# One product per 128 tokens in a gated recurrence, and a reordered opening, in a two-block transformer kernel

## The chip, the cores and the metric

The kernel runs on one core of one Trainium2 chip. The metric is device microseconds of one execution: 2290.91, the median of three runs (2289.15 to 2291.92). The engines are TensorE (matrix products; PE in the rows, its weight loads PEld), VectorE (DVE), ScalarE (ACT), GpSimd (POOL) and SyncE (SP, which issues most loads). TensorE writes to PSUM, in banks of 128 x 512 fp32; ScalarE and VectorE read it from there.

## The reference

One sequence of 512 tokens, width 1024, passes through two blocks in fp32. The first block has a normalised input projection, a differential attention (4 heads of two 64-wide halves, rotary positions, block-causal mask) beside a banded attention (8 heads), a cross attention to 256 memory tokens and a gated feed-forward stage. The second has a top-k attention with a gating branch, a feed-forward stage with a short convolution, a gated linear recurrence (8 heads), and another such feed-forward stage. Two parts matter here:

```
q, k = rope(z[q cols]), rope(z[k cols])      # x1*cos - x2*sin, x2*cos + x1*sin
attn = softmax(q0 k0') - lam * softmax(q1 k1');  out = attn @ v

# recurrence, per chunk of 64 tokens, state S (128 x 128), b = cumsum(log g)
inter = (q * exp(b)) @ S
a[t,s] = sum_d q[t,d] * exp(b[t,d] - b[s,d]) * k[s,d]   for s <= t, else 0
out = a @ i + inter
S = exp(b_last) * S + (k * exp(b_last - b))' @ i
```

## The kernel before

Activations are kept transposed, features on the 128 partitions and the 512 tokens along the free dimension, in eight tiles. Each weight product is done in three passes of TensorE's rounded fp32 type (`mm3`, L131 to L133): activation and weight are split into a high and a low half, and high x high, high x low and low x high are summed in one PSUM bank. ScalarE makes the high half of a weight tile of 128 x 1024 (`whi`, L118), VectorE the low half (`wlo`, L119); two of each are kept, and three raw tiles (`wraw`), which SyncE loads 512 KB at a time. A step of a product generator (`fm`, features out, one bank for 24 products when its head is 1; `tm512`, tokens out) is three products. Weight products use four PSUM banks (`pg`).

A planner orders each engine's instructions when the kernel is built: by its own estimate of time it takes, of what is ready, what comes first in the program; work in a `high_priority` block comes ahead of other work, and `issue_after(ins)` keeps work behind an instruction on that instruction's engine. Attention and recurrence heads are written as generators whose stages are advanced one per round by `pipeline` (from L397 on); after each round `fill` issues some steps of the generators in `self.line`, so that weight products lie between the dependent stages.

The opening is `mix`. It splits x into halves (`xg`), sums the squares (`sumsq`, L235 for the sums, L229 for squares on GpSimd, L231 for squares on ScalarE), and starts the query products (four tiles, four banks at once). After 16 steps, column sums give the mean square (`pst`, L244), GpSimd its inverse root (`rs`, L260), and two products its broadcast (`psb`, L286). The evacuation of a query or key tile, `rope`, has four ScalarE copies of 32 partitions out of PSUM (L497), a product with cos (L498), a product with sin on GpSimd (L499), a sum (L500), then casts and differences into halves (`pack_q` L418 and L419, `pack_k` L429 and L430). Then come four key tiles, then the values (`tm512`), small constants and the bias of the second attention on GpSimd's DMA queue, and then 16 attention steps, each with scores, softmax, transposes and a product with the values. The filler of these is the second attention's values, its queries and keys, and the gate.

The recurrence is `recur`. For each head, six levels of masked scores are put together in a buffer `abuf` of two halves (one per head in turn): its lower and upper 64 partitions hold the two 64x64 diagonal blocks of each group of 128 tokens, all groups in 4 x 64 columns. The scores of the second chunk with the first (L1142) come from PSUM. ScalarE puts these and the upper diagonal blocks into a tile `B` (128 x 256, L1146 and L1147). The state is updated (`pu`, L1161), and the output product is one uninterrupted run of TensorE instructions per head (L1171, L1172, L1174): fp32 products, each of which the profile records as two. TensorE is given its operands by tile shape (rows x columns of its array), which the rows name as 64*64, 128*64 or 128*128.

Of the kernel before, what the change touches and what calls it, by code (L numbers as in the profile page):

```python
# [8 lines left out]
F32 = mybir.dt.float32  # L9
# [4 lines left out]
ALU = mybir.AluOpType  # L14
AX = mybir.AxisListType

P = 128
# [52 lines left out]
class Kern:  # L70
# [400 lines left out]
    def mix(self):  # L471
        nc, d = self.nc, self.d
        xs = [self.u(f"x{k}", "x") for k in range(KT)]
        w = d["w_in"]
# [10 lines left out]
        op = [self.split(xs[k], "xg", self.col("norm_mix_g", k)) for k in range(KT)]  # L485
        self.more_consts()
        cos, sin = self.u("cos", "c"), self.u("sin", "c")
        nc.sync.dma_start(cos, d["cos"])
        nc.sync.dma_start(sin, d["sin"])
        acc = self.sumsq(xs, sq_eng=nc.gpsimd)  # L490
        qa, ka = [], []

        def rope(dst, pack):
            def evac(n, ps):
                r, sw = self.u("rope", "y"), self.u("sw", "a")
                for b in range(0, P, 32):
                    nc.scalar.copy(sw[b:b + 32], ps[b ^ 32:(b ^ 32) + 32])  # L497
                nc.vector.tensor_tensor(r, ps, cos, op=ALU.mult)  # L498
                self.pmul = nc.gpsimd.tensor_tensor(sw, sw, sin, op=ALU.mult).ins  # L499
                nc.vector.tensor_tensor(r, r, sw, op=ALU.add)  # L500
                dst.extend(pack(r))
            return evac

        def tok(dst, nm):
            def evac(j, ps):
                t = self.u(nm, "g")
                nc.scalar.activation(t, ps, AF.Identity, scale=rst[:, j:j + 1])
                dst[j] = t
            return evac
# [7 lines left out]
            nc.gpsimd.tensor_tensor(t, t, rsb, op=ALU.mult)  # L517
        self.run(first)
        va = [None] * 4
        self.run(self.fm(w[4:8], op, rope(ka, lambda z: self.pack_k(z, "g"))))  # L520
        self.run(self.tm512(w[8:12], op, tok(va, "va")))

        lv = self.u("lv", "a")[:, :256]
        nc.sync.dma_start(lv, bass.AP(tensor=d["lam"].tensor, offset=d["lam"].offset, ap=[[0, P], [1, 256]]))
# [12 lines left out]
        nc.vector.tensor_scalar(g8, self.col("subln"), 1.0 - lam_init, None, op0=ALU.mult)  # L537

        e0, e1 = self.u("ext", "a")[:8, :384], self.u("ext", "a")[:8, :384]
        with self.tc.issue_after(self.pmul):  # L540
            nc.gpsimd.dma_start(e0[:, 383:384], d["rbr"][:, 0:1])
            nc.gpsimd.dma_start(e1, d["rbr"][:, 1:385])
        nc.vector.tensor_copy(e0[:, 0:383], e0[:, 383:384].to_broadcast([8, 383]))
# [8 lines left out]
        def step(h, i):  # L552
            W = P * (i + 1)
            if i == 0:
                st[h, "r0"] = self.small("r0", 4)
            r0 = st[h, "r0"]
            zs = [self.pad_q(qa[2 * h + c], 64 * c, i) for c in range(2)]
            yield
            es, sm = [], self.small("sm2", 2)
            mx = self.small("mx2", 2)  # L560
            for c in range(2):
                ps = self.ps.tile([P, T], F32, name="psa", tag="ps")
                self.score(ps, qa[2 * h + c], ka[2 * h + c], zs[c], i, W, False)
                nc.tensor.matmul(ps[:, W - CUT:W], self.identb, self.corner, start=False, stop=True)
                nc.vector.tensor_reduce(mx[:, c:c + 1], ps[:, :W], axis=AX.X, op=ALU.max)
                nc.vector.tensor_scalar(mx[:, c:c + 1], mx[:, c:c + 1], -0.125, None, op0=ALU.mult)
                e = self.u("ea", "a")
                nc.scalar.activation(e[:, :W], ps[:, :W], AF.Exp, bias=mx[:, c:c + 1], scale=0.125,
                                     accum_out=sm[:, c:c + 1])
                es.append(e)  # L570
            rc = self.small("rc2", 2)
            nc.vector.reciprocal(rc, sm)
            nc.vector.tensor_copy(r0[:, i:i + 1], rc[:, 0:1])

            cf = self.small("cf", 1)
            nc.vector.scalar_tensor_tensor(cf, rc[:, 1:2], nlam, sm[:, 0:1], op0=ALU.mult, op1=ALU.mult)
            at = es[0]
            nc.vector.scalar_tensor_tensor(at[:, :W], es[1][:, :W], cf, es[0][:, :W], op0=ALU.mult, op1=ALU.add)
            yield
            pt = self.pt.tile([P, T], F32, name="pta", tag="pt")  # L580
            for j in range(i + 1):
                nc.tensor.transpose(pt[:, j * P:j * P + P], at[:, j * P:j * P + P], self.ident)
            aT = self.u("aT", "a")
            nc.scalar.copy(aT[:, :W], pt[:, :W])
            yield
            if i == 0:
                st[h, "po"] = self.po.tile([P, T], F32, name="poa", tag="po")
            po = st[h, "po"]
            for j in range(i + 1):
                nc.tensor.matmul(po[:, i * P:i * P + P], aT[:, j * P:j * P + P], va[j][:, h * P:h * P + P],  # L590
                                 start=j == 0, stop=j == i)
            if i == 3:
                o = self.u("oa", "a")
                r3 = lambda a: a.rearrange("p (i e) -> p i e", i=4)
                nc.vector.tensor_tensor(r3(o), r3(po), r0[:, :, None].to_broadcast([P, 4, P]), op=ALU.mult)
                self.head_norm(o, 4)
                yield
                yield
                yah[h] = self.to_feature(o, "ya", g8)

        qb, kb, vb = [None] * 8, [None] * 8, [None] * 4
# [12 lines left out]
        def gate(which, tag):  # L614
            def evac(n, ps):
                z = self.u("zg", tag[n])
                nc.vector.tensor_tensor(z, ps, rsb, op=ALU.mult)
                nc.scalar.activation(z, z, AF.Tanh, scale=0.5)
                tg[which, n] = z
            return evac  # L620
# [11 lines left out]

        ybh = [None] * 4
        qk = self.fm(w[16:24], op, heads)
        self.line = [self.tm512(w[12:16], op, tok(vb, "vb")), qk, self.fm(w[24:32], op, gate("a", "g" * 8))]
        self.pipeline([step(h, i) for h in range(4) for i in range(4)], RATE["a"])
        self.finish(qk)
        self.line += [self.fm(d["w_up_a"], yah, merge("a")),
# [395 lines left out]
    def recur(self, xs):  # L1034
        nc, d = self.nc, self.d
        op = [self.split(xs[k], "hg", self.col("mix1", k)) for k in range(KT)]
        acc = self.sumsq(xs)
        w = d["c_in"]
# [23 lines left out]
        abuf = self.u("abuf", "c")  # L1062
        with self.tc.issue_after(self.rs):
            nc.gpsimd.memset(abuf, 0.0)

        it = {}
        on = [None] * 8
# [15 lines left out]
        def grow(ks, qs, dec, m):  # L1083

            v4 = lambda t: t.rearrange("p (n a m) -> p n a m", a=2, m=m)
            d2 = dec.rearrange("p (n a) -> p n a", a=2)
            w = [P, T // (2 * m), m]
            nc.vector.tensor_tensor(v4(ks)[:, :, 0], v4(ks)[:, :, 0], d2[:, :, 1:2].to_broadcast(w), op=ALU.mult)
            nc.vector.tensor_tensor(v4(qs)[:, :, 1], v4(qs)[:, :, 1], d2[:, :, 0:1].to_broadcast(w), op=ALU.mult)

        def head(h):
            hc = slice((h % 4) * P, (h % 4) * P + P)
            itok = [it[h // 4, j][:, hc] for j in range(4)]
# [6 lines left out]
            g = zf  # L1100
# [8 lines left out]
            dec, at, w = [g], 0, T  # L1109
# [8 lines left out]
            A = abuf[:, (h % 2) * 256:(h % 2) * 256 + 256]  # L1118
            for lv in range(7):
# [4 lines left out]
                n = 32 if lv else 64  # L1124
                ps = self.ps.tile([P, T], F32, name="pl", tag="ps")
                for c in range(8):
                    r, s = (c % 2) * 64, slice(c * 64, c * 64 + 64)
# [7 lines left out]
                else:  # L1135
                    r3 = lambda t: t.rearrange("p (j t) -> p j t", j=4)
# [3 lines left out]
            ps = self.ps.tile([P, T], F32, name="pl", tag="ps")  # L1140
            for j in range(4):
                nc.tensor.matmul(ps[:64, j * 64:j * 64 + 64], ks[:, j * P:j * P + 64], qs[:, j * P + 64:j * P + P],  # L1142
                                 start=True, stop=True)
            yield
            B = self.u("B", "a")[:, :256]
            nc.scalar.copy(B[:64], ps[:64, :256])  # L1146
            nc.scalar.copy(B[64:], A[64:])  # L1147
            grow(ks, qs, dec[6], 64)
            yield
            pt = self.pt.tile([P, T], F32, name="ptk", tag="pt")  # L1150
# [8 lines left out]
            for j in range(3):  # L1159
                s = slice(j * P, j * P + P)  # L1160
# [4 lines left out]
                                               op0=ALU.mult, op1=ALU.add)  # L1165
            yield
            po = self.po.tile([P, T], F32, name="poh", tag="po")
            lo, hi = slice(0, 64), slice(64, P)
            for j in range(4):
                s, t = slice(j * P, j * P + P), slice(j * 64, j * 64 + 64)  # L1170
                nc.tensor.matmul(po[lo, s], A[lo, t], itok[j][lo], start=True, stop=j == 0)  # L1171
                nc.tensor.matmul(po[hi, s], B[:, t], itok[j], start=True, stop=j == 0)  # L1172
                if j:
                    nc.tensor.matmul(po[:, s], qs[:, s], sl(j), start=False, stop=True)  # L1174
            o = self.u("ho", "y")
# [33 lines left out]
        def heads(h):  # L1209
            self.finish(ti[h // 4])  # L1210
            self.finish(fq[h])
            yield from head(h)
            out_head(h)
# [187 lines left out]
```

## Time and profile before

| what | value |
|---|---|
| median of three runs | 2290.91 us |
| profiled execution | 2289.7 us |
| its span, first to last instruction | 2287.9 us |
| VectorE busy | 1390.4 us, 61% |
| ScalarE busy | 912.3 us, 40% |
| GpSimd busy | 272.0 us, 12% |
| mean granted TensorE clock | 0.991 |

Busy time of TensorE is that of products in a pipeline whose ends are modelled: a product of 512 columns is shown with 0.39 us where the next one starts 0.23 later. So the cost of a product is read from the starts of two that follow each other. Idle times count only where the engine had nothing else to do, and "released by" names the instruction that came last.

### The profile page before, as it was taken

Reading aid. Unit: us, or ns where it says so; the run is one execution under the profiler, and the core shown is the slowest. Engines: PE = TensorE matmul, PEld = TensorE weight load, DVE = VectorE, ACT = ScalarE, POOL = GpSimd, SP = SyncE. Lnnn points to the kernel's source line nnn. Section 1 sums busy time; section 2 is a strip of 40 time slices with the busy share of each in tenths; the row PEclk is TensorE's granted clock in tenths of the full one; section 3 lists DMA queues with packets and bytes.
Section 4 is the critical chain, followed back from the end, with each engine's and each line's share of the span. In section 5 each row is a group of like instructions: output and inputs, shape, how many; then the busy total and the mean of one; then the engine's idle time right before and its main releaser. Section 6 shows DMA issues by size and latency. Waiting matters only on the chain.

```text
span 2287.9 us, 28921 instructions
## 1 busy us (share of the span) xinstructions
PE 2226.7 (97%) x11254; PEld 1808.5 (79%) x11254; DVE 1390.4 (61%) x2391; ACT 912.3 (40%) x1426; POOL 272.0 (12%) x360
## 2 busy tenths in 40 slices
PE   7899999999999999998999999999999999999997
PEld 6778777888888888777678888888877778888886
DVE  7576556766444333589876877633456646777534
ACT  5454443544323222462553544422322234444322
POOL 4212200000111100123230000000112210000001
PEclk9999999999999999999999999999999999999999
DMA  4423323522533333313213333333212123333333
GB/s 143 99 64 94 93 74 102 160 71 76 106 98 96 99 95 100 103 47 95 67 56 92 94 100 95 99 95 101 84 56 65 56 65 93 98 96 99 95 99 104
DMA packets 62536, 207.28 MB, mean 91 GB/s; under 512 B 8216, under 2 KB 12384, under 8 KB 62400
## 3 DMA queue, kind: packets, MB, share of 16 engines
q1 hardware_dynamic: 58368, 198.60, 28.7%
q0 software_dynamic: 2880, 5.79, 1.6%
q8 instruction: 88, 1.44, 0.3%
q10 hardware_dynamic: 1152, 1.05, 0.1%
q14 instruction: 48, 0.39, 0.1%
HBM read 201.74 MB, written 3.67 MB: 90 GB/s over the span
## 4 chain that ended last, share of the span: by engine, by line
PE 86%; DVE 9%; ACT 2%; issue 1%; POOL 1%; DMA 0%; SPq 0%; DVEq 0%; ACTq 0%; POOLq 0%
PE pg L131 26%; PE pg L132 25%; PE pg L133 25%; PE pl L1128 1%; DVE isc L925 1%; DVE wlo L119 1%; PE po L390 1%; DVE m L924 1%; PE ptr L378 1%; ACT whi L118 1%; DVE qhl L419 1%; DVE khh L429 1%; DVE isc L915 1%; PE poh L1172 1%; PE poh L1171 1%
## 5 line engine op out<-in xcount | busy, mean ns | idle before, releaser
L118 ACT CAST whi<-wraw 128x1024 fp32r<-128x1024 f32 (+1 forms) x368 | 386.0, 1049 | 737.6 <-PE pg L132 458.9
L119 DVE TENSOR_TENSOR wlo<-wraw,whi 128x1024 fp32r<-128x1024 f32 (+1 forms) x356 | 436.7, 1227 | 320.4 <-ACT whi L118 314.4
L131 PE MATMUL pg<-fg2h,whi 128*128 128x512 f32 x704 | 274.1, 389 | 0.0
L133 PE MATMUL pg<-fg2h,wlo 128*128 128x512 f32 x704 | 273.9, 389 | 0.0
L132 PE MATMUL pg<-fg2l,whi 128*128 128x512 f32 x704 | 273.9, 389 | 0.0
L131 PEld LDWEIGHTS pg<-fg2h,whi 128*128 128x128 f32 x704 | 132.2, 188 | 27.4
L133 PEld LDWEIGHTS pg<-fg2h,wlo 128*128 128x128 f32 x704 | 132.2, 188 | 27.4
L132 PEld LDWEIGHTS pg<-fg2l,whi 128*128 128x128 f32 x704 | 132.2, 188 | 27.4
L133 PE MATMUL pg<-m2h,wlo 128*128 128x512 f32 (+1 forms) x374 | 140.9, 377 | 0.6 <-DVE wlo L119 0.6
L131 PE MATMUL pg<-m2h,whi 128*128 128x512 f32 (+1 forms) x374 | 141.0, 377 | 0.0
L132 PE MATMUL pg<-m2l,whi 128*128 128x512 f32 (+1 forms) x374 | 140.8, 376 | 0.0
L131 PE MATMUL pg<-fgh,whi 128*128 128x512 f32 x352 | 137.3, 390 | 0.9 <-ACT whi L118 0.9
L133 PE MATMUL pg<-fgh,wlo 128*128 128x512 f32 x352 | 137.1, 389 | 0.0
L132 PE MATMUL pg<-fgl,whi 128*128 128x512 f32 x352 | 137.0, 389 | 0.0
L1021 DVE SCALAR_TENSOR_TENSOR yc<-zc,vecs,yc 128x511 f32<-128x511 f32 (+1 forms) x176 | 130.8, 747 | 2.7
L260 POOL TENSOR_TENSOR rs<-ms,mhalf 128x4 f32<-128x4 f32 (+1 forms) x11 | 12.0, 1090 | 943.4 <-DVE ms L247 585.1
L131 PE MATMUL pg<-xgh,whi 128*128 128x512 f32 x256 | 103.9, 406 | 7.1 <-ACT xgh L217 5.9
L1017 DVE TENSOR_TENSOR zc<-pg,rsb 128x512 f32<-128x512 f32 x88 | 60.5, 688 | 74.1 <-PE pg L133 74.1
L132 PE MATMUL pg<-xgl,whi 128*128 128x512 f32 x256 | 101.9, 398 | 0.5 <-DVE xgl L218 0.5
L133 PE MATMUL pg<-xgh,wlo 128*128 128x512 f32 x256 | 101.2, 395 | 0.0
L133 PEld LDWEIGHTS pg<-m2h,wlo 128*128 128x128 f32 x374 | 70.3, 188 | 13.6 <-DVE wlo L119 0.8
L131 PEld LDWEIGHTS pg<-m2h,whi 128*128 128x128 f32 x374 | 70.3, 188 | 13.0
(424 smaller groups left out, 4812.6 us busy)
## 6 DMA issues: line engine op xcount, KB each, us to landing
wraw<-in_ffn_up SPq DMA_DIRECT2D x88, 512.0 KB, 3.5
wraw<-in_ffn_down SPq DMA_DIRECT2D x48, 512.0 KB, 3.5
wraw<-in_w_gate_up SPq DMA_DIRECT2D x44, 512.0 KB, 3.5
wraw<-in_w_in SPq DMA_DIRECT2D x39, 512.0 KB, 3.6
wraw<-in_c_in SPq DMA_DIRECT2D x32, 512.0 KB, 3.5
wraw<-in_ab SPq DMA_DIRECT2D x29, 512.0 KB, 3.6
wraw<-in_w_down SPq DMA_DIRECT2D x22, 512.0 KB, 3.5
wraw<-in_w_ckv SPq DMA_DIRECT2D x16, 512.0 KB, 4.1
```

What stands on the lines that cost most here:

```text
L118: nc.scalar.copy(hi[:, p], raw[:, p])
L119: eng.tensor_tensor(lo[:, p], raw[:, p], hi[:, p], op=ALU.subtract)
L131: mm(out, w[0], x[0], start=start, stop=False)
L132: mm(out, w[0], x[1], start=False, stop=False)
L133: return mm(out, w[1], x[0], start=False, stop=stop).ins
L378: nc.tensor.transpose(pt[:, j * P:j * P + P], es[a][:, j * P:j * P + P], self.ident)
L390: nc.tensor.matmul(po[r, i * P:i * P + P], v[j][:, c0:c0 + 64], pts[a][:, j * P:j * P + P], start=j == 0, stop=j == i)
L419: self.nc.vector.tensor_tensor(t[b:b + 64], z[a:a + 64], t[a:a + 64], op=ALU.subtract)
L429: (self.nc.scalar.copy if a == b else self.nc.vector.tensor_copy)(t[b:b + 64], z[a:a + 64])
L915: nc.vector.scalar_tensor_tensor(a[:, :W], r[:, :W], s, a[:, :W], op0=ALU.mult, op1=ALU.add)
L1017: nc.vector.tensor_tensor(z, ps, rsb, op=ALU.mult)
L1021: nc.vector.scalar_tensor_tensor(y[:, sh:], z[:, :T - sh], self.col(f"cw{l}{j}", f), y[:, sh:], op0=ALU.mult, op1=ALU.add)
```

## The change

In the recurrence, a tile `AB` of 128 x 4 x 128 (two of them, for heads in turn, with one quadrant cleared once) replaces `B`. Three ScalarE copies put the two diagonal blocks and the block between them in place, and one 128x128 product per group replaces a 64x64 and a 128x64 one.

In the opening, the squares go from GpSimd to ScalarE. The evacuation of query and key tiles is put at high priority, and its product with sin goes from GpSimd to VectorE. The values are produced right behind the queries, then the first key tile; the other three key tiles become filler of the attention rounds. A head's first step makes sure that its key tile is issued. Two small loads on GpSimd's queue are tied to the inverse root in place of the rotary product.

```diff
-        acc = self.sumsq(xs, sq_eng=nc.gpsimd)
-        qa, ka = [], []
+        acc = self.sumsq(xs)
+        qa, ka = [None] * 8, [None] * 8
...
-                for b in range(0, P, 32):
-                    nc.scalar.copy(sw[b:b + 32], ps[b ^ 32:(b ^ 32) + 32])
-                nc.vector.tensor_tensor(r, ps, cos, op=ALU.mult)
-                self.pmul = nc.gpsimd.tensor_tensor(sw, sw, sin, op=ALU.mult).ins
-                nc.vector.tensor_tensor(r, r, sw, op=ALU.add)
-                dst.extend(pack(r))
+                with self.tc.high_priority():
+                    for b in range(0, P, 32):
+                        nc.scalar.copy(sw[b:b + 32], ps[b ^ 32:(b ^ 32) + 32])
+                    nc.vector.tensor_tensor(r, ps, cos, op=ALU.mult)
+                    nc.vector.tensor_tensor(sw, sw, sin, op=ALU.mult)
+                    nc.vector.tensor_tensor(r, r, sw, op=ALU.add)
+                    dst[2 * n:2 * n + 2] = pack(r)
...
-        self.run(self.fm(w[4:8], op, rope(ka, lambda z: self.pack_k(z, "g"))))
+        keys = [self.fm(w[4 + p:5 + p], op, rope(ka, lambda z: self.pack_k(z, "g")), p) for p in range(4)]
         self.run(self.tm512(w[8:12], op, tok(va, "va")))
+        self.run(keys[0])
...
-        with self.tc.issue_after(self.pmul):
+        with self.tc.issue_after(self.rs):
...
             if i == 0:
+                self.finish(keys[h])
...
-        self.line = [self.tm512(w[12:16], op, tok(vb, "vb")), qk, self.fm(w[24:32], op, gate("a", "g" * 8))]
+        self.line = keys[1:3] + [self.tm512(w[12:16], op, tok(vb, "vb")), keys[3], qk,
+                                 self.fm(w[24:32], op, gate("a", "g" * 8))]
...
+            ab = [self.cp.tile([P, 4, P], F32, name=f"ab{n}") for n in range(2)]
+            for t in ab:
+                nc.gpsimd.memset(t[64:, :, :64], 0.0)
...
-            B = self.u("B", "a")[:, :256]
-            nc.scalar.copy(B[:64], ps[:64, :256])
-            nc.scalar.copy(B[64:], A[64:])
+            AB = ab[h % 2]
+            r3 = lambda t: t.rearrange("p (j t) -> p j t", j=4)
+            nc.scalar.copy(AB[:64, :, 64:], r3(ps[:64, :256]))
+            nc.scalar.copy(AB[:64, :, :64], r3(A[:64]))
+            nc.scalar.copy(AB[64:, :, 64:], r3(A[64:]))
...
-                s, t = slice(j * P, j * P + P), slice(j * 64, j * 64 + 64)
-                nc.tensor.matmul(po[lo, s], A[lo, t], itok[j][lo], start=True, stop=j == 0)
-                nc.tensor.matmul(po[hi, s], B[:, t], itok[j], start=True, stop=j == 0)
+                s = slice(j * P, j * P + P)
+                nc.tensor.matmul(po[:, s], AB[:, j], itok[j], start=True, stop=j == 0)
```

## Rows read from the trace of the kernel before

**Rows 1.** The page, busy time by engine: us, share, instructions.
```profile
PE 2226.7 (97%) x11254; PEld 1808.5 (79%) x11254; DVE 1390.4 (61%) x2391; ACT 912.3 (40%) x1426; POOL 272.0 (12%) x360
```
**Rows 2.** Waits of TensorE, whole span: who for whom, us in total, times, longest.
```profile
PE pst L244 <- DVE sq L235: 3.9, 1, 3.9
PE pg L132 <- DVE wlo L119: 3.9, 3, 2.2
PE pg L131 <- DVE rope L498: 3.7, 2, 2.5
```
**Rows 3.** Stretches: length, busy us and count of PE, PEld, DVE, ACT, POOL; clock; DMA.
```profile
26.00:32.00 6.00, 6.00 (x20) 4.96 (x21) 3.17 (x15) 0.22 (x1) 1.01 (x1) 0.60 0.31 91
40.00:60.00 20.00, 20.00 (x88) 16.56 (x89) 15.75 (x21) 18.74 (x32) 9.08 (x12) 1.00 0.27 79
60.00:80.00 20.00, 13.88 (x48) 10.32 (x47) 18.64 (x32) 12.66 (x20) 6.30 (x6) 0.83 0.31 72
96.00:130.00 34.00, 32.87 (x177) 27.17 (x176) 18.37 (x56) 15.47 (x38) 5.91 (x14) 1.00 0.38 90
1632.00:1700.00 68.00, 67.10 (x575) 52.40 (x574) 43.62 (x91) 15.10 (x22) 14.88 (x26) 1.00 0.24 71
```
**Rows 4.** Timeline of TensorE, output products of the first and last head: start, us.
```profile
1675.17 0.39 PE L133 MATMUL pg<-whi,hgl 128*128 128x512 f32 x1
1675.49 0.43 PE L1171 MATMUL poh<-itok,abuf 64*64 64x128 f32 x2
...
1676.94 0.49 PE L1174 MATMUL poh<-S,qs 128*128 128x128 f32 x2
1677.36 0.43 PE L1171 MATMUL poh<-itok,abuf 64*64 64x128 f32 x2
...
1679.63 0.66 PE L1128 MATMUL pl<-qs,ks 128*64 128x32 f32 x16
...
1863.24 0.43 PE L1171 MATMUL poh<-itok,abuf 64*64 64x128 f32 x2
...
1867.21 0.48 PE L131 MATMUL pg<-yhh,whi 128*128 128x512 f32 x1
```
**Rows 5.** Timeline of TensorE, state update of the first head and what follows.
```profile
1670.52 0.83 PE L1161 MATMUL pu<-itok,kst 128*128 128x128 f32 x6
1671.28 0.66 PE L1128 MATMUL pl<-qs,ks 128*64 128x32 f32 x16
```
**Rows 6.** Instructions of tile B: durations in ns (least, median, most), starts, forms.
```profile
L1147 ACT COPY B<-abuf x8: 402/402/408, 1653.1 to 1853.5; 64x256 f32<-64x256 f32 x8
```
**Rows 7.** Timeline of TensorE in the opening, around the column sums and the queries' end.
```profile
20.83 0.39 PE L131 MATMUL pg<-xgh,whi 128*128 128x512 f32 x1
25.17 1.87 PE L244 MATMUL pst<-ones,sq 128*128 128x1 f32 x8 [3.95 <-DVE sq L235]
...
38.36 0.39 PE L133 MATMUL pg<-xgh,wlo 128*128 128x512 f32 x1
39.93 0.50 PE L131 MATMUL pg<-xgh,whi 128*128 128x512 f32 x1 [1.18 <-DVE rope L498]
```
**Rows 8.** Squares: on GpSimd (tile sq, opening), on ScalarE (by line, whole span).
```profile
L229 POOL TENSOR_TENSOR sq<-x x8: 1165/1494/1956, 5.1 to 21.5; 128x512 f32<-128x512 f32 x8
...
L231 ACT ACTIVATE sq<-x 128x512 f32<-128x512 f32 x48 | 28.7, 619 | 2.3 <-DVE sq L235 2.3
```
**Rows 9.** ScalarE by line, 36 to 60 us: busy us, mean ns, idle before.
```profile
L497 ACT COPY sw<-pg 32x512 f32<-32x512 f32 x24 | 13.9, 578 | 2.9 <-PE pg L133 2.5
L418 ACT CAST qhl<-rope 64x512 fp32r<-64x512 f32 x8 | 5.0, 619 | 0.9 <-DVE rope L500 0.7
L118 ACT CAST whi<-wraw 128x1024 fp32r<-128x1024 f32 x3 | 3.1, 1048 | 0.0
```
**Rows 10.** VectorE by line, 36 to 80 us.
```profile
L430 DVE TENSOR_TENSOR kl<-rope,khh 64x512 fp32r<-64x512 f32 x8 | 5.9, 733 | 0.2
L498 DVE TENSOR_TENSOR rope<-pg,cos 128x512 f32<-128x512 f32 x8 | 5.5, 689 | 3.9 <-ACT sw L497 3.7
```

More of the change, by code (lines that the diff above doesn't have):

```diff
@@ L1167, in head @@
             po = self.po.tile([P, T], F32, name="poh", tag="po")
-            lo, hi = slice(0, 64), slice(64, P)
             for j in range(4):
-                s, t = slice(j * P, j * P + P), slice(j * 64, j * 64 + 64)
-                nc.tensor.matmul(po[lo, s], A[lo, t], itok[j][lo], start=True, stop=j == 0)
-                nc.tensor.matmul(po[hi, s], B[:, t], itok[j], start=True, stop=j == 0)
+                s = slice(j * P, j * P + P)
+                nc.tensor.matmul(po[:, s], AB[:, j], itok[j], start=True, stop=j == 0)
                 if j:
```

## The prediction

> **What bounds the kernel now.** I read the busy times first: TensorE is busy for 97% of the span, no other engine for more than 61% [rows 1]. Next came the list of what TensorE waited for. Its rows for the opening are short ones: 3.9 us for the sum of squares, 3.9 us in three waits for the low halves of weights, 3.7 us in two waits for rotary products to let go of a PSUM bank [rows 2]. So time is to be had in two ways: fewer TensorE microseconds where it never waits, or those waits and the clock that falls after them. Then the stretches: in the recurrence (1632 to 1700 us) TensorE is busy 67.1 of 68 us at full clock, with VectorE at 43.6 and ScalarE at 15.1 [rows 3]. In the opening the granted clock is 0.60 in 26 to 32 us and 0.83 in 60 to 80 us, where it is 1.00 in the rest of what is shown: the lower of the two levels (1.2 GHz) for part of these stretches, each time behind a stretch in which TensorE stood still [rows 3, 7]. Last came the order of instructions on TensorE at the two places that the change edits [rows 4, 5, 7], and the durations of what moves [rows 6, 8 to 10].
>
> The sum is made against the profiled execution, 2289.7 us (span 2287.9 and 1.8 around it). It lies 1.2 below the median of the three runs, 2290.91; I put the difference on that median.
>
> **Recurrence: products.** Per head the output product is issued as one block. For each of four groups of 128 tokens it has a 64x64 product (L1171), a 128x64 product (L1172) and, in three groups, the 128x128 product with the state (L1174). Each is two records. The first head's block starts at 1675.49 and the next work starts at 1679.63: 4.14 us. The last head's goes from 1863.24 to 1867.21: 3.97 us [rows 4]. The six between show 4.14 or 4.15, so eight blocks are 7 x 4.14 + 3.97 = 32.95 us. In front of the block TensorE also loses a little: the full product at 1675.17 needs 0.23, the block comes 0.32 behind it, so 0.09 x 8 = 0.7. After the change a block has seven products, all 128x128 with 128 columns in fp32 (four of the score tile, three of the state). The nearest row is the state update of the same stage, three products of just that form: from 1670.52 to the start of the following work at 1671.28, 0.76 us, so 0.253 each with the change of shape at the end in it [rows 5]. Seven are 1.77, eight blocks 14.2. Gain: 32.95 + 0.7 - 14.2 = 19.5 us.
> Bounds: if every product were spaced like the state product that now stands before a smaller one, 0.42 (1676.94 to 1677.36) [rows 4], a block were 2.94 and the gain 9.4 (without the 0.7). If 0.16 of the 0.76 is the change of shape, a product is 0.20, a block 1.56 and the gain 21.2. I take 19.5, since rows 5 have the form itself.
> Is it on the path? TensorE has 0.9 us of idle in 68 there [rows 3], so what goes from it goes from the span. A round that had a block loses 2.4 us of cover for the other engines, but stays longer by 1.8 than the rounds without one, which have their cover now.
> The rows show the two half-width products of a group one behind the other (8 of them and 3 whole ones in 4.14). The Trainium skill, page "TensorEngine Tiling (Array Packing)", section "Tiling Modes", says that different tiles of the array can load weights and multiply in parallel; by that a 64x64 and a 128x64 product on different columns would share their time, and the sum would lose this whole term. The trace does not agree, with 4.14 for the block where seven whole products would be 1.77.
>
> **Recurrence: the rest.** Two ScalarE copies of 64x256 become three; the one from the score buffer takes 0.40 [rows 6], so 8 x 0.40 = 3.2 us more on ScalarE, which is busy 15.1 of 68 us there [rows 3]: hidden; without that cover at most 3.2. The third copy waits for the same last masked write as the copy before it did, and queued behind it on ScalarE are casts of weights, which have a chunk in hand. Two clears on GpSimd, done once, far ahead: nothing. Together 0 to +3; I take 0.
>
> **Opening: squares.** Eight squares of 1.49 us (median) on GpSimd become eight of 0.62 on ScalarE [rows 8]. TensorE runs dry at 21.06 (the product of 20.83 and its 0.23), starts the column sums at 25.17 and ends the query products at 38.36 + 0.23 = 38.59 [rows 7]: 17.5 us. At full clock a product takes 0.227 (88 in the 20 us from 40 to 60) [rows 3], and that work is 47 products, 10.7, two broadcasts 0.5 and eight column sums 0.8: 12.0. So up to 5.5 us is there, 4 of waiting and the rest half clock. ScalarE does the squares (L231) in all later norms, and in the whole run TensorE waits for squares this one time [rows 2, 8]. I take 5.2; the bounds are 0 (the sums still end at 25) and 5.5.
>
> **Opening: what follows the queries.** Before, the keys came next: one PSUM bank per 24 products. Now the values come next, and they want four banks within four times six products, 1.36 us each, while all four banks hold queries. A bank comes free after four ScalarE copies of 0.578 and one VectorE product of 0.69; with priority on the whole evacuation, ScalarE also does the two casts of a tile (0.62 each) ahead of the copies of later tiles [rows 9, 10]. Counted from the end of the first query tile (the queries end 2.04 later): copies of tile 0 until 2.4, of 1 until 4.75, casts of tile 0 until 6.0, copies of 2 until 8.3, casts of 1 until 9.55, copies of 3 until 11.9. Banks are free at 3.1, 5.4, 9.0 and 12.6, and the fourth group of products ends at 14.0 in place of 2.04 + 5.44 = 7.5: 6.5 us lost. The next weights' cast (1.05) comes behind that, for 1.5 us more: 8.0, where before 1.2 was lost [rows 7]. So +6.8. Bounds: with the copies alone in front, the fourth bank at 10.1, +2.8; with low halves late as well, +9.
> In return the keys' own waits go. In 60 to 80 us TensorE ran 48 products, 10.9 us at full clock; of the 9.1 lost, 6.1 were standing still (busy 13.9 of 20), at low halves and at a bank, the longest waits 2.2 and 2.5 [rows 2, 3], and 3.0 the clock. I count -6.1, and leave the clock at 0: it will fall once in the new stall as it did in the old.
> The products themselves (72 of the three key tiles) only move; they displace other filler, which comes later. Their 512 KB weight loads move with them in SyncE's queue: the values' four loads pass the keys' four, the number is the same. The two small loads on GpSimd's queue leave their place behind the rotary product for one behind the first inverse root, ahead of the mask copies: nothing.
>
> **Opening: the first scores.** They need the first key tile: four copies (2.3), two products and a sum on VectorE (2.1), two casts and a difference (1.9): 6.3 us, against five filler steps of three products, 3.4 us. 2.9 is exposed if TensorE has nothing else; the planner may put later filler in front. I take +0.7, between 0 and 2.9.
> **The other three key tiles** bring VectorE some 4.3 us each and ScalarE 3.6 [rows 9, 10] into the rounds from 96 us on, where they are busy 18.4 and 15.5 of 34 us and TensorE idles 1.1 [rows 3]. Both stay below the span (31 and 26 of 34); I take +0.6 for late softmax steps, between 0 and 4. The rotary product on VectorE (0.69 in place of GpSimd's) is in these sums.
>
> Opening: -5.2 + 6.8 - 6.1 + 0.7 + 0.6 = -3.2. In all -19.5 - 3.2 = -22.7: 2290.9 - 22.7 = 2268.
>
> **The rivals.**
> (a) Forecast, 2268, by itself 2263 to 2273: chance 0.50.
> (b) The new bank waits are small (+2.8), the clock does not fall (-3.0), squares come fully in time: opening -12, 2259. For: the evacuation has priority now. Against: ScalarE's 11.9 us of copies and casts are the same work. 0.14.
> (c) The opening is worse: +9 at the banks, 2.9 at the first scores, 4 in the rounds, squares half in time (-2.7): +7, 2278. For: late low halves cost 3.9 before. 0.18.
> (d) The whole products are spaced at 0.42: gain 9.4 with the opening as forecast, 2278. For: rows 4 show it. Against: there a smaller shape follows. 0.11.
> (e) The half-width products already run beside each other on different columns, and the records only show their latency: then a block costs as much after as before, and only the opening is left, 2288. Against: the next work starts 4.14 behind the block's start [rows 4], and latency would not add up. 0.02. (The page named above has this rule of the Trainium skill.)
> (f) The slower one: ScalarE. Its rotary copies now stand ahead of the casts of weights by priority, from the queries to the last key tile; if each of the chunks cast in that time comes late by the longest wait for a low half seen before, 2.2 us [rows 2], eleven chunks cancel the 22.7, and the fourteen from the values to the last key tile and the first pairs give 31: 2299. For: three such waits before. Against: ScalarE is busy less than half of 96 to 130 us. 0.03.
> That the merged product is not there at all I leave out: the code names one product per group.
>
> **How the numbers follow.** A measurement here tells about 0.2% (4.6 us) from no change. Faster: (a) to (d) and a little, 0.94. Same: (e) and some of (f), 0.03. Slower: 0.03. The range takes in (a), most of (b) and of (c) and (d): 2259 to 2279.
>
> **What would show it.** Right: blocks of L1174 and the merged product near 1.8 us from first record to next work, eight times; no wait of TensorE for squares, and the column sums near 21 us; a wait of several microseconds at the first products of the values, behind rotary products. Wrong: blocks near 3 us; waits of TensorE for VectorE in the recurrence's rounds that were not there; the values' products without a wait, or low halves late again and again after 40 us.

## The result, and the profile after

The changed kernel takes 2265.81 us (median, 2264.45 to 2266.82), against 2290.75 for the kernel before: ratio 0.9892, 95% interval 0.9876 to 0.9907. Its profiled execution takes 2266.8 us. The forecast was 2268, within 2259 to 2279.

The page after answers to [rows 1]: busy time of TensorE fell by 20.6 us, the share stayed.

```profile
span 2264.7 us, 28799 instructions
PE 2206.1 (97%) x11186; PEld 1797.1 (79%) x11190; DVE 1386.7 (61%) x2399; ACT 917.4 (41%) x1442; POOL 251.2 (11%) x346
```

**Recurrence.** TensorE's timeline of the first and last head's block after the change (start, us), for [rows 4]:

```profile
1670.62 0.39 PE L133 MATMUL pg<-whi,hgl 128*128 128x512 f32 x1
1670.85 0.60 PE L1180 MATMUL poh<-itok,ab 128*128 128x128 f32 x4
1671.29 0.39 PE L1182 MATMUL poh<-S,qs 128*128 128x128 f32 x2
...
1672.50 0.66 PE L1135 MATMUL pl<-qs,ks 128*64 128x32 f32 x16
...
1843.33 0.60 PE L1180 MATMUL poh<-itok,ab 128*128 128x128 f32 x4
...
1844.81 0.48 PE L131 MATMUL pg<-yhh,whi 128*128 128x512 f32 x1
```

A block is 1.65 us (seven of 1.65 or 1.66, the last 1.48) and comes 0.23 behind the full product ahead of it. All eight are 13.05 us where 32.95 stood, and 0.7 of lead-in is gone: 20.6 us.

The stage, from the first product with tokens out to the last head's, in the kernel before and after (columns as in [rows 3]):

```profile
1594.00:1870.00 276.00, 273.34 (x2045) 212.84 (x2044) 160.42 (x319) 80.43 (x117) 57.02 (x81) 1.00 0.21 64
```
```profile
1590.00:1848.00 258.00, 253.44 (x1981) 207.58 (x1980) 160.16 (x319) 83.60 (x125) 57.07 (x81) 1.00 0.23 68
```

TensorE is idle 4.6 us of it after and 2.7 before: 1.9 us came back as waits. The waits of TensorE in that stretch after (who for whom, us, times, longest); the first line is new, the others were there:

```profile
PE pl L1135 <- DVE abuf L1140: 1.9, 5, 0.6
PE pl L1135 <- DVE qs L1096: 1.7, 2, 0.9
PE ptk L1162 <- DVE zg L1209: 0.9, 1, 0.9
```

So the stage is about 18 us shorter, not 20.6.

**Opening.** TensorE's waits of the opening after, up to 80 us, from its timeline, with the column sums among them, for [rows 7]. The first line is the first product of all, which came 0.6 us later in this execution than in that of the kernel before (5.93):

```profile
6.53 0.80 PE L131 MATMUL pg<-xgh,whi 128*128 128x512 f32 x1 [6.53 <-ACT xgh L217]
21.31 1.05 PE L244 MATMUL pst<-ones,sq 128*128 128x1 f32 x8
26.65 0.50 PE L286 MATMUL psb<-dg,onesr 128*128 128x512 f32 x1 [0.51 <-DVE dg L275]
40.69 0.80 PE L131 MATMUL pg<-whi,xgh 128*128 128x512 f32 x1 [6.70 <-DVE rope L499]
76.95 0.30 PE L445 MATMUL psa<-khh,qhl 128*128 128x128 f32 x1 [0.38 <-ACT khh L429]
```

The wait for squares is gone: the column sums start at 21.3 us where they started at 25.2. The three waits between 60 and 80 us are gone too. One wait of 6.7 us stands behind the queries, for a rotary product. The stretches for [rows 3], with the one around that wait:

```profile
26.00:32.00 6.00, 5.49 (x24) 4.43 (x24) 4.14 (x9) 1.64 (x3) 2.80 (x2) 1.00 0.31 90
36.00:47.00 11.00, 6.31 (x16) 4.97 (x17) 7.50 (x13) 6.50 (x13) 0.78 (x1) 0.53 0.16 48
60.00:80.00 20.00, 19.62 (x88) 15.70 (x86) 9.30 (x16) 10.52 (x15) 0.71 (x1) 1.00 0.29 87
96.00:130.00 34.00, 33.27 (x177) 25.27 (x177) 20.06 (x60) 16.77 (x40) 4.17 (x13) 1.00 0.26 79
```

The granted clock is at its upper level in 26 to 32 and 60 to 80 us now, and mostly at its lower one in 36 to 47, behind the wait: the 16 products there are 3.6 us of work at full clock and took 6.3. In 96 to 130 us, with the key tiles as filler, TensorE is idle 0.7 us where it was 1.1. The cross attention's first products on this block's result start 4.2 us earlier than before (449.0 in place of 453.2), or 4.8 counted from the first product of all: that is the opening's gain in this execution.

Why the wait is one of 6.7 us is in two rows of ScalarE and the first of VectorE, from their timelines:

```profile
31.99 2.25 ACT L498 COPY sw<-pg 32x512 f32<-32x512 f32 x4 [2.55 <-PE pg L133]
34.15 1.04 ACT L118 CAST whi<-wraw 128x1024 fp32r<-128x1024 f32 x1
35.09 6.20 ACT L498 COPY sw<-pg 32x512 f32<-32x512 f32 x12
```
```profile
39.95 0.69 DVE L499 TENSOR_TENSOR rope<-pg,cos 128x512 f32<-128x512 f32 x1 [3.50 <-ACT sw L498]
```

A tile needs four copies, and the first four are over at 34.2. But the first rotary product, which frees the first bank, starts at 39.95, when the ninth of the following twelve is through. In the instruction list of the changed program the copies are not tile after tile: two of the first query tile, then one of each tile in turn, and the first tile's last copy is the thirteenth of sixteen.

### The profile page after: what moved, and what is told of

The parts are those of the page before. It is cut to its first block, busy times and chain, and to the rows that moved or that the text cites. A ratio compares the mean times of both kernels' runs of the same rounds, so it can differ in the third digit from the quotient of the medians.

```text
span 2264.7 us, 28799 instructions
## 1 busy us (share of the span) xinstructions
PE 2206.1 (97%) x11186; PEld 1797.1 (79%) x11190; DVE 1386.7 (61%) x2399; ACT 917.4 (41%) x1442; POOL 251.2 (11%) x346
## 3 DMA queue, kind: packets, MB, share of 16 engines
HBM read 201.74 MB, written 3.67 MB: 91 GB/s over the span
## 4 chain that ended last, share of the span: by engine, by line
PE 86%; DVE 8%; ACT 2%; issue 1%; POOL 1%; DMA 0%; DVEq 0%; SPq 0%; ACTq 0%; POOLq 0%
PE pg L131 26%; PE pg L132 26%; PE pg L133 26%; PE pl L1135 1%; DVE isc L929 1%; DVE m L928 1%; PE ptr L378 1%; DVE wlo L119 1%; PE po L390 1%; ACT whi L118 1%; ACT sw L498 1%; POOL rs L260 1%; DVE isc L919 1%; DVE qhl L419 1%; DVE khh L429 0%
## 5 line engine op out<-in xcount | busy, mean ns | idle before, releaser
L132 PEld LDWEIGHTS pg<-m2l,whi 128*128 128x128 f32 x374 | 70.3, 188 | 13.0
```

Source lines behind the costliest of these rows:

```text
L132: mm(out, w[0], x[1], start=False, stop=False)
```

## Experiments

All times are medians beside runs of the kernel before; ratios are to that, with 95% intervals.

**The two parts alone.** e1_recur is the kernel before with `recur` of the changed one, e2_open the kernel before with the changed `mix`, e3_squares the kernel before with one line changed:

```diff
-        acc = self.sumsq(xs, sq_eng=nc.gpsimd)
+        acc = self.sumsq(xs)
```

> The kernel before with the recurrence's part of the change alone. Theory (the parts add up, and blocks of output products are the gain): the trace of the changed kernel shows blocks of 1.65 us where 4.14 stood, 20.6 us less, of which 2 to 3 come back as waits; so 17.8 below the kernel before, ratio 0.9922, 2273. Rival (the parts are not separate: the recurrence also moved because the opening shifted the planner's order): less than 15 or more than 21.

> The kernel before with the opening's part of the change alone. Theory (additive): 4 to 5 us below the kernel before, ratio about 0.998, 2286; one wait of 6.7 us for a rotary product behind the queries, and the clock at its lower level from then to about 46 us. Rival: the opening alone is no gain, because what it brings depends on the recurrence: within 1 us.

> The kernel before with its squares on ScalarE and nothing else. Theory (the step of the prediction: 5.2): the 3.9 us wait of the column sums is gone and the granted clock stays at its upper level in 24 to 31 us; 5 us below the kernel before, 2286. Then all else in the opening is worth nothing net. Rival 1: ScalarE's and VectorE's copies and casts behind the queries come no earlier, and the wait only moves to the first key products: 0 to 2 us. Rival 2: ScalarE is late with the weights' casts: slower.

Measured: e1_recur 2271.44, ratio 0.9923 (0.9908 to 0.9938); e2_open 2283.58, 0.9970 (0.9960 to 0.9980); e3_squares 2283.28, 0.9975 (0.9966 to 0.9984). The first two multiply to 0.9893, the change's own 0.9892: the parts add up, some 17.6 us (14.2 to 21.1) and 6.9 (4.6 to 9.2). The squares alone give 5.7 (3.7 to 7.8). So all that else was done in the opening gave nothing that these runs can tell from zero. In e3_squares the granted clock is at its upper level in 24 to 31 us, and the waits at the keys are the old ones, five microseconds earlier:

```profile
24.00:31.00 7.00, 6.47 (x29) 5.04 (x28) 5.41 (x13) 1.64 (x2) 2.78 (x2) 1.00 0.26 78
```
```profile
34.96 0.50 PE L131 MATMUL pg<-xgh,whi 128*128 128x512 f32 x1 [1.18 <-DVE rope L498]
58.60 0.50 PE L132 MATMUL pg<-wlo,xgh 128*128 128x512 f32 x1 [1.36 <-DVE wlo L119]
65.20 0.50 PE L132 MATMUL pg<-wlo,xgh 128*128 128x512 f32 x1 [2.17 <-DVE wlo L119]
68.48 0.79 PE L131 MATMUL pg<-whi,xgh 128*128 128x512 f32 x1 [2.55 <-DVE rope L498]
```

**What the 6.7 us wait is.** e4_key_first swaps two lines of the changed kernel:

```diff
-        self.run(self.tm512(w[8:12], op, tok(va, "va")))
         self.run(keys[0])
+        self.run(self.tm512(w[8:12], op, tok(va, "va")))
```

> The changed kernel with the first key tile issued ahead of the values (two lines swapped). Theory A (the four tiles' copies out of PSUM are issued in turn, one of each tile, so that no bank comes free before nearly all sixteen are done): the wait behind the queries stays at 6 to 7 us, now at the first key product, the clock falls as it did, and the time is within 2 us of the changed kernel. Theory B (the wait comes of the values' need for four banks, as the prediction had it): the first key product waits about 1.2 us, the values little, the clock does not fall, and the time is 6 to 8 us below the changed kernel.

Measured: 2262.66, ratio 0.9883 (0.9868 to 0.9898), not to be told from the changed kernel's. The wait stays, with a key tile behind it that needs one bank:

```profile
40.36 0.80 PE L131 MATMUL pg<-xgh,whi 128*128 128x512 f32 x1 [6.69 <-DVE rope L499]
```

Theory A holds and the prediction's picture falls: it is not the values' need of four banks, no bank is free before. The stretch from 34 to 47 us has 17 products and the lower clock:

```profile
34.00:47.00 13.00, 6.64 (x17) 5.24 (x18) 8.58 (x14) 8.22 (x16) 1.10 (x1) 0.61 0.19 59
```

**Copies tile by tile.** e8_tile_by_tile is e4_key_first with this; e9_tile_values has it with the values first again:

```diff
+                    with self.tc.issue_after(self.swap) if self.swap else nullcontext():
                         for b in range(0, P, 32):
-                            nc.scalar.copy(sw[b:b + 32], ps[b ^ 32:(b ^ 32) + 32])
+                            c = nc.scalar.copy(sw[b:b + 32], ps[b ^ 32:(b ^ 32) + 32])
+                    self.swap = c.ins
```

> The changed kernel with the first key tile ahead of the values, and with each tile's four copies out of PSUM tied behind the last copy of the tile before it. Theory A (the wait comes of copies taken in turn from all four tiles): the first key product waits 1 to 2 us in place of 6.7, the clock does not fall behind it (2.5 to 3 us more), the values find their banks free: 7 to 9 below the kernel that has the key first alone, 2254 to 2256. Rival (ScalarE's sixteen copies and eight casts are one amount of work and bound the stretch in any order): the waits come back at the values or the first scores, within 2 us of the kernel that has the key first.

> The changed kernel (values first) with each tile's four copies tied behind the last copy of the tile before it. Theory A: banks come free one by one some 2.4 us apart, so the values' first four groups wait about 1, 1, 1 and 1 us in place of 6.7 at once; the clock may stay: 3 to 6 below the changed kernel, 2260 to 2263. Rival (ScalarE's work bounds the stretch): 6 to 8 us of waits in sum, spread, and no gain. The step of the prediction (casts of earlier tiles ahead of copies of later ones, 6.5 lost) would be seen as waits of 1, 1, 2 and 2 us.

Measured: e8_tile_by_tile 2256.52, ratio 0.9847 (0.9830 to 0.9863), below the changed kernel's interval; e9_tile_values 2261.85, 0.9871 (0.9856 to 0.9886). TensorE's waits in e8_tile_by_tile behind the queries, and the same stretch, are:

```profile
34.66 0.50 PE L132 MATMUL pg<-xgh,whi 128*128 128x512 f32 x1 [1.18 <-DVE rope L502]
44.30 0.50 PE L132 MATMUL pg<-whi,xgh 128*128 128x512 f32 x1 [0.95 <-DVE rope L502]
46.14 0.50 PE L132 MATMUL pg<-whi,xgh 128*128 128x512 f32 x1 [0.17 <-DVE rope L502]
```
```profile
34.00:47.00 13.00, 11.21 (x47) 8.65 (x48) 11.03 (x16) 12.66 (x21) 0.86 (x2) 1.00 0.32 97
```

2.3 us of waits in place of 6.7, the clock at its upper level, and 47 products in 13 us where e4_key_first had 17: Theory A, though 6 us below e4_key_first where it gave 7 to 9. In e9_tile_values the waits at this place are 1.2 us for a bank and 0.6 and 0.4 for low halves, and the clock stays up too. It is 5 us behind e8_tile_by_tile: half of that is in TensorE's waits up to the cross attention (2.5 us more in sum, at transposes and first scores), half is open.

**Priority and place.** e5_noprio is the changed kernel without the `high_priority` block of `rope`; e10_gpsin has the product with sin on GpSimd again; e11_keys_all is e8_tile_by_tile with all keys ahead of the values and none as filler:

```diff
-                with self.tc.high_priority():
...
-                    nc.vector.tensor_tensor(sw, sw, sin, op=ALU.mult)
+                    nc.gpsimd.tensor_tensor(sw, sw, sin, op=ALU.mult)
...
-        self.run(keys[0])
+        self.run(*keys)
```

> The changed kernel without high priority for the evacuation of query and key tiles (values first, rotary product on VectorE as in the change). Theory (priority for several tiles at once is what makes the planner take their copies in turn): the copies come tile by tile again, the 6.7 us wait behind the queries splits into waits of about 1 us, but casts of weights and softmax work stand ahead of the evacuation: 2 to 5 below the changed kernel, 2261 to 2264. Rival 1 (the order is the same without priority, ready work being taken as it comes): the 6.7 us wait stays, no difference. Rival 2 (without priority the key tiles come late to the scores): waits at scores, slower than the changed kernel.

> The changed kernel with the product with sin back on GpSimd (1.4 in place of 0.69 us a tile). Theory (the banks do not wait for that product, and the chain to the first scores has only 0.4 us exposed): 0 to 1.5 us above the changed kernel, the first scores waiting about 1 us. Rival (GpSimd beside VectorE slows VectorE's own work, and the fillers' key tiles delay the softmax): 3 us or more above.

> The kernel of e8 (tile by tile, key first), but all four key tiles come ahead of the values, none as filler. Theory (a key tile keeps VectorE busy 4.3 us and a weight tile 1.2, 5.5 in all against TensorE's 5.44, so they only just keep up): waits of TensorE of 1 to 3 us in sum for banks or low halves, and 1 to 3 us above e8, 2258 to 2260; the filler's part of the change is worth that much. Rival (in the old place they cost what they cost before, 6.1 and the clock's 3.0): 8 to 9 above e8. Rival 2 (their place is worth nothing once the order is right): within 1 us of e8.

Measured: e5_noprio 2259.91, ratio 0.9865 (0.9848 to 0.9881); e10_gpsin 2265.85, 0.9890 (0.9875 to 0.9905); e11_keys_all 2263.46, 0.9880 (0.9866 to 0.9895).

Without the priority the wait of 6.7 is gone, as the theory had it, and in the program's instruction list the copies stand tile after tile, as in the kernel before; the first four groups of the values wait 1.2, 0.2, 0.5 and 0.7 us, and the clock does not fall:

```profile
34.60 0.50 PE L131 MATMUL pg<-whi,xgh 128*128 128x512 f32 x1 [1.18 <-DVE rope L498]
37.98 0.50 PE L131 MATMUL pg<-whi,xgh 128*128 128x512 f32 x1 [0.22 <-DVE rope L498]
41.53 0.50 PE L131 MATMUL pg<-whi,xgh 128*128 128x512 f32 x1 [0.54 <-DVE rope L498]
45.21 0.50 PE L131 MATMUL pg<-whi,xgh 128*128 128x512 f32 x1 [0.65 <-DVE rope L498]
```

So the priority that the change adds costs it these microseconds; the intervals of the two kernels still touch, and the trace decides. The rotary product's engine is worth nothing: with GpSimd the first scores wait 1.2 us in place of 0.4, and the time is the same.

The place of the three key tiles is worth 7 us, more than the theory's 1 to 3 and nearly the first rival's 8 to 9: in e11_keys_all, the values behind four key tiles wait 4.0 us for a bank, and the clock falls.

```profile
65.73 0.79 PE L132 MATMUL pg<-whi,xgh 128*128 128x512 f32 x1 [4.01 <-DVE rope L502]
```
```profile
62.00:72.00 10.00, 6.27 (x17) 5.00 (x18) 9.64 (x15) 5.15 (x9) 0.00 (x0) 0.66 0.19 52
```

VectorE is busy 9.6 of the 10 us there: it falls behind TensorE over four key tiles in a row, and the bill comes at the values. The 17 products there are 3.9 us at full clock and took 6.3, so the clock cost 2.4 more.

**What a block's product costs.** e6_half issues each merged product of the changed kernel as two of 64 columns; e7_alternate reorders the products of the kernel before (`one` is the 64x64 product of a group, `two` the 128x64 one):

```diff
-                nc.tensor.matmul(po[:, s], AB[:, j], itok[j], start=True, stop=j == 0)
+                for a in (0, 64):
+                    nc.tensor.matmul(po[a:a + 64, s], AB[:, j, a:a + 64], itok[j], start=True, stop=j == 0)
...
+                if j == 2:
+                    nc.tensor.matmul(po[:, s], qs[:, s], sl(j), start=True, stop=False)
+                for m in (one, two) if j % 2 else (two, one):
+                    nc.tensor.matmul(*m, start=j != 2, stop=j in (0, 2))
```

> The changed kernel, but each merged product is issued as two of 64 columns (same score tile, upper and lower half of the output), so a head's block again has eleven products, with fewer changes of tile shape than before. Theory (a product costs 0.211 whatever its width and each change of shape 0.165; from 1.48 = 7 products, 1.65 with one change, 4.14 = eleven products and eleven changes): 11 x 0.211 + 6 x 0.165 = 3.3 us a block, 13 us above the changed kernel, 2279. Rival 1 (a half-width product costs 0.36 by itself): 4.1 us a block, 20 above, 2285. Rival 2 (products on different columns run beside each other, the rule of the Trainium skill's page on tiling): seven products' time and six changes, 2.5 us a block, 7 above, 2272.

> The kernel before with the same eleven products of a block in another order (groups alternate between both half products first and last), so that three of eleven changes of tile shape fall away and nothing else. Theory (0.165 per change of shape): blocks of 3.64 in place of 4.14 us, 4 us below the kernel before, ratio 0.998. Rival (the price lies in the half-width products, not in the change): blocks of 4.1, no difference.

Measured: e6_half 2272.19, ratio 0.9916 (0.9901 to 0.9930), blocks of 2.58 us (the last 2.40); e7_alternate 2286.79, 0.9984 (0.9975 to 0.9994), blocks of 3.66 or 3.67 (the last 3.49). Blocks of the first head, e6_half and e7_alternate:

```profile
1670.64 0.66 PE L1181 MATMUL poh<-itok,ab 128*64 128x128 f32 x8
1671.23 0.49 PE L1183 MATMUL poh<-S,qs 128*128 128x128 f32 x2
1671.65 0.44 PE L1181 MATMUL poh<-itok,ab 128*64 128x128 f32 x4
1672.02 0.49 PE L1183 MATMUL poh<-S,qs 128*128 128x128 f32 x2
...
1673.22 0.66 PE L1135 MATMUL pl<-qs,ks 128*64 128x32 f32 x16
```
```profile
1678.31 0.43 PE L1176 MATMUL poh<-itok,B 128*64 128x128 f32 x2
1678.67 0.65 PE L1176 MATMUL poh<-itok,abuf 64*64 64x128 f32 x4
1679.25 0.43 PE L1176 MATMUL poh<-itok,B 128*64 128x128 f32 x2
...
1681.97 0.54 PE L1128 MATMUL pl<-qs,ks 128*64 128x32 f32 x12
```

e7_alternate bears out the price of a change of shape: three fewer, 0.48 less a block, 0.16 each. e6_half refutes the other half of that theory and fits Rival 2: the four half products of the first two groups (x8) take 0.59 with a change of shape in it, two of a later group (x4) 0.37, so a pair more costs 0.22, and the first records of a pair start 0.006 to 0.007 us apart. Two products on different columns do run beside each other if their shape is the same. In e7_alternate the two 64x64 products, on the same columns, take 0.58 with a change: 0.21 each, so a half-width product by itself is no cheaper than a whole one. e6_half also loses the wait for masked writes: with blocks of 2.58 us TensorE's list of waits no longer has it, while e1_recur, with blocks of 1.65, has 1.9 us of it in five waits.

**Filler in the recurrence.** e12_rate is e8_tile_by_tile with this:

```diff
-RATE = {"a": 5.7, "b": 5, "x": 3.5, "i": 1, "s": 1.6, "d": 2, "h": 4.5}
+RATE = {"a": 5.7, "b": 5, "x": 3.5, "i": 1, "s": 1.6, "d": 2, "h": 5}
```

> The kernel of e8 with 5 in place of 4.5 filler steps between the recurrence's rounds. Theory (the 1.9 us of new waits for masked writes and part of the rest of the 2.8 us that the shorter blocks gave back come of rounds now too short for VectorE): these waits go, 1 to 2 us below e8. Rival (the filler is used up sooner, and the last heads stand without cover): as e8 or 1 to 3 us above.

Measured: 2256.59, ratio 0.9849 (0.9834 to 0.9864): no difference from e8_tile_by_tile, as the rival had it. The waits of masked scores are now:

```profile
PE pl L1138 <- DVE abuf L1143: 1.7, 3, 0.9
PE pl L1138 <- DVE qs L1099: 0.6, 1, 0.6
```

The new waits that the theory wanted gone are still 1.7 us where they were 1.9; the old ones fell from 1.7 to 0.6, and others (1.0 at the weight products behind the last head, 0.2 at transposes) came for them.

The kernel that beats both is e8_tile_by_tile: 34 us below the kernel before, 9 below the changed one.

## Why the prediction came out right

- **Recurrence, -19.5.** Right in kind and nearly in size: e1_recur measured -17.6, the stage in the trace -18. The blocks gave 20.6, because a product took 0.21 where I had 0.253 with the change of shape spread over three. What I missed is the 1.9 us of new waits: I wrote that what goes from TensorE goes from the span, and a shorter block left masked writes uncovered in five rounds (they are covered again with the longer blocks of e6_half).
- **The rule on tiles.** I set it aside because the two half products of a group stood one behind the other. That they did is what counted for the sum, but the reason was another: their shapes differed. Where they agree, as in e6_half, the trace agrees with the Trainium skill, "TensorEngine Tiling (Array Packing)", section "Tiling Modes", on different tiles in parallel (0.22 us a pair), and with its sentence there that a change of mode drains the engine (0.16 us each here), which the prediction left out. Of the 2.5 us that a block lost, 0.93 is what e6_half's block has above the merged one; the rest could have been had with two half products of one shape.
- **Squares, -5.2.** e3_squares: -5.7 (3.7 to 7.8). Right by wait and by clock, but not by its sum: from 21.06 to 38.59 us the trace has 41 products of weights, not 47, so that up to 6.9 us was there and not 5.5. In the trace of e3_squares the queries end 5.2 us earlier, counted from the first product of all; a wait of 0.5 for a broadcast stays, and the clock first rises 2.1 us later in that execution. That TensorE waits for squares only once in the run was misread too: the last norm has another such wait (1.2 us, L1255), with its squares on ScalarE.
- **Behind the queries, +6.8.** Of 8.0 lost, less the 1.2 from before, the trace has 6.7 less 1.2: 5.5. The further 1.5 us for the next weights' cast did not come. The rest was nearly met in size (6.5 foretold), but by another mechanism, and that is chance. I let banks come free 2.3 to 3.6 us apart, with casts of earlier tiles ahead of copies of later ones; in fact the sixteen copies went in turn and nothing was free until the thirteenth (e4_key_first, e8_tile_by_tile).
- **Keys' waits, -6.1, and the clock at 0.** Both as forecast: the waits are gone, and the clock fell once in the new stall (2.7 us by the rows of 36 to 47 us) as in the old (3.0). e11_keys_all shows what the move is worth once the copies go tile by tile: 7 us. (Of the three waits for low halves that I put to the opening one stands at 447 us; it is not in the 6.1.)
- **First scores +0.7 and rounds +0.6.** The first scores wait 0.4. The rounds lost nothing: TensorE is idle 0.4 us less in 96 to 130 us, and its waits from 80 us to the cross attention sum to 5.0 us where they were 5.9.
- **The sum.** The opening in all was put at -3.2; e2_open says -6.9 (4.6 to 9.2). In the traces it is 6.4 for e2_open and 4.8 for the changed kernel, both counted from the first product of all; behind the stall the clock was low for 6.8 us in the one and for 10.2 in the other. By the medians of e1_recur and e2_open the recurrence was put too high by 1.9 and the opening too low by 3.7; that these cancel in part is luck.
- **The rivals.** (d) with products at 0.42 and (e) are out by the blocks of 1.65, (c) by e2_open's gain; (f), low halves late chunk after chunk, did not happen. (b) did not happen either: the waits were not small. Its small bank waits and steady clock are what e8_tile_by_tile shows.

## What to carry to other kernels

A product's price is read from the start of the next, and a change of tile shape between two products has a price of its own: count shapes in a sequence as well as products. When a block gives several independent chains the same high priority, look at the order in which the chains are taken: interleaved, the first result comes almost as late as the last, and what waits for the first (here a PSUM bank) waits for all. And a wait behind which the clock falls costs more than itself: 2.7 us on top of 6.7 in the changed kernel, 2.4 on top of 4.0 in e11_keys_all.

## What the hardware showed that I had not expected

Two fp32 products of 64 output columns each, on different columns and with the same 128x64 shape, took 0.22 us together, about as one of 128 columns does (0.21), while two of different shapes took 0.36 each with the change. The clock's fall in a wait of 6.7 us cost 2.7 us more, and the waits of 0.2 to 1.2 us that took its place in e5_noprio and e8_tile_by_tile did not drop it. In e3_squares, as in the kernel before, it fell during the second of two waits of 2.2 and 2.55 us with 0.7 us of products between them.
